# Four stages of a two-layer sequence mixer rearranged: gate columns, forms of h, decay products, adaLN rest

## The chip, the core and the metric

The kernel runs on one core of a Trainium2 chip. The metric is the device time of one execution in microseconds (us). TensorE (PE) multiplies, VectorE (DVE), ScalarE (ACT) and GpSimd (POOL) work element by element, SyncE (SP) issues transfers; GpSimd issues some transfers too, in line with its own instructions. Each engine takes its instructions in a fixed order and waits at the first whose inputs are not there.

## The reference

Two layers of a hybrid mixer over 512 latent and 256 context tokens of width 1024, batch 1, in float32. Each layer: RMSNorm, shift and scale from SiLU(c) (adaLN), one input projection `u = h @ w_in + b_in` whose columns feed two branches and the merge gates, then

```python
rq, rk, rv, rz, mq, mk, mv, mo, mz, mg, gr, gm = split(u)   # 1024 columns each, mg 32
# retention, 8 heads of 128, chunks of 128 tokens, both directions
scores = einsum(qc, kc) * dmat;  inner = scores @ vc
cross  = (qc @ s_prev) * xi                 # xi: the decay of a token in its chunk
# mLSTM, 8 heads of 128, both directions, running-max stabiliser
y_r = headnorm(ret) * silu(rz) @ w_ro;  y_m = headnorm(ml) * silu(mz) @ w_mo
x = x + gate * ((sigmoid(gr) * y_r + sigmoid(gm) * y_m) @ w_out)
```

Latent scans start from the final state of the context. A last RMSNorm gives the output of the latent tokens.

## The kernel before

Every float32 operand of a matmul is split into a high and a low part (`h_hi`, `h_lo`; `w_hi`, `w_lo` in two neighbouring slots of w0 to w3), and a product is three matmuls: high by high, high by low, low by high. A split is a copy by ScalarE (line 180) and a difference by VectorE (line 181), or, for weights under `wsplit`, two ScalarE passes (lines 192, 193) and an accumulating transfer on GpSimd's queue (line 194).

A layer runs through these stages. **gm**: four gate pairs, `gmp{layer}_{j}_256` for the latent and `_0` for the context tokens, each from a pair of weight blocks (gm0, gm2, gm4, gm6) and followed by a tanh on ScalarE into `gmt` (line 621). **Strassen**: the columns of the queries, keys and merge gates as block products `sx`, `sy`, `sz` (line 725). `sy` and `sz` need the forms `t12`, `t34` (sums and differences of four blocks of h), which `make_forms` builds: it loads `fa` and `fb` back from DRAM, forms `fc` and `fd` on VectorE (lines 646 to 649) and splits them. **Retention**: `rvg` (line 281) gives the values of head 0 and 1 and 32 gate columns; `rv0_p` the other values; for each head `rk` (transposes, line 1016), `rs` (scores), the products of queries by decay `xi` into `ws3` (line 1079), `rkv`, `ro`, then `yt_r` (line 1032). **mLSTM**: the same with `mk`, `ms`, `mo`, `yt_m`; the matmuls `mv` (line 274) are its values. Gate columns `gr` (merge gate of the retention branch, in pairs) are spread over these heads: `GRP` says after which retention pair, `GRH` at which mLSTM heads, the rest come after the mLSTM. **br, bm, ou**: branch outputs times gates, and the output projection.

The adaLN parameters (shift, scale, gate: 24 blocks of 128 for each layer) are computed by matmuls at the start for what layer 0 needs first; the rest, `ada_rest`, by VectorE: a block of `in_wadat` is loaded on GpSimd's queue (line 371, four buffers), multiplied by the two rows of SiLU(c) and summed along the row (line 388, result `adj` thrown away, sum kept). For layer 0 blocks 16 to 23 this runs in the retention, in `ws3`, in steps of 256 columns: 8 x 4 steps with two products each, 64 products. For layer 1 it runs after the mLSTM in `gwf`, in steps of 512 columns.

The order is made in two levels. Generators in the list `main` are advanced by `tick()`, those in `side` (the `ada_rest`) by `aside(n)` by n steps, and `drain` runs a list to its end; so calls between the matmul loops decide what is issued where. Over that, a scheduler that works with priorities orders each engine's instructions; code under `tc.high_priority(offset=LOWP)`, with LOWP = -200, is put off.

Of the kernel before, what the change touches and what calls it, by code (L numbers as in the profile page):

```python
# [26 lines left out]
KB = 8  # L27
# [10 lines left out]
LOWP = -200  # L38
# [2 lines left out]
POS = [0, 3, 1, 2, 4, 5]  # L41
KO = [0, 4, 1, 5, 2, 6, 3, 7]
GRP = [(2,), ()]
GRH = [(2, 5), ()]
CTX = slice(0, NCTX)
LAT = slice(NCTX, T)
ROWS = (slice(0, 32), slice(32, 64))
# [18 lines left out]
def build(tc, io):  # L66
# [3 lines left out]
    with ExitStack() as es:  # L70
# [24 lines left out]
        def chunks(t, n=NCH):  # L95
            return t.rearrange("p (n c) -> p n c", n=n)
# [37 lines left out]
        def ensure(key):  # L134
            while key not in finished:
                tick(False)
# [313 lines left out]
        for l in range(NL):  # L450
            def pair(name, a, b, summed=0):
                spec(f"{name}_{l}", wb[l, a], wb[l, b], summed=summed)
            for j in range(0, 8, 2):
                pair(f"gm{j}", B_GM + j, B_GM + j + 1, 2 if j else 0)

            def gr(p):
                pair(f"gr{p}", B_GR + 2 * p, B_GR + 2 * p + 1)
            for p in range(4):
                if p:
                    pair(f"rv{p}", B_RV + 2 * p, B_RV + 2 * p + 1)  # L460
                else:
                    spec(f"rvg_{l}", io["wrvg"][l])
                if l == NL - 1:
                    pair(f"rz{p}", B_RZ + 2 * p, B_RZ + 2 * p + 1)
                    pair(f"rq{p}", B_RQ + 2 * p, B_RQ + 2 * p + 1)
                if p in GRP[l]:
                    gr(GRP[l].index(p))
            if l == NL - 1:
                pair("mq0", B_MQ, B_MQ + 1)
            for h in range(H):  # L470
                pair(f"vo{h}", B_MV + h, B_MO + h)
                if l == NL - 1 and h % 2 == 0:
                    pair(f"mv{h}", B_MV + h, B_MV + h + 1)
                    pair(f"mz{h}", B_MZ + h, B_MZ + h + 1)
                if h in GRH[l]:
                    gr(len(GRP[l]) + GRH[l].index(h))
                if l == NL - 1 and h % 2 and h < H - 1:
                    pair(f"mq{h + 1}", B_MQ + h + 1, B_MQ + h + 2)
            for p in range(len(GRP[l] + GRH[l]), 4):
                gr(p)  # L480
            for nm, summed in (("wro", 2 - 2 * l), ("wmo", 2 - 2 * l), ("wout", 0), ("wout", 0)):
                for p in range(4):
                    spec(f"{nm}{p}_{l}", io[nm][l, 2 * p], io[nm][l, 2 * p + 1], summed=summed)
# [26 lines left out]
        def modulate_ctx(l, x, rst, hp):  # L510
            for i, kb in enumerate(KO):
                modulate(l, x, rst, hp, CTX, kb)
                if i % 3 == 2:
                    yield

        def start_ctx():
            for kb in range(KB):
                square_add(acc, xin[:, kb], kb, CTX)
            rstd_rows(acc, rst, CTX, "ms_inc")
            yield from modulate_ctx(0, xin, rst, hp)  # L520
        main.append(start_ctx())
# [12 lines left out]
        for l in range(NL):  # L534
# [100 lines left out]


            def make_forms(sl):
                n = 256 if sl is LAT else P
                c0 = P if sl is LAT else 0
                for k in range(4):  # L640
                    t0, t1 = stage(f"fa{l}_{k}_{n}"), stage(f"fb{l}_{k}_{n}")
                    for t, kb in ((t0, k), (t1, k + 4)):
                        nc.sync.dma_start(t[:, :2 * n], hd[l][kb][:, sl])
                    (a0, b0_), (a1, b1_) = [(t[:, 0:n], t[:, n:2 * n]) for t in (t0, t1)]
                    f12, f34 = stage(f"fc{l}_{k}_{n}"), stage(f"fd{l}_{k}_{n}")
                    v.tensor_tensor(f12[:, 0:n], b0_, a0, op=OP.subtract)
                    v.tensor_tensor(f12[:, n:2 * n], b1_, f12[:, 0:n], op=OP.subtract)
                    v.tensor_tensor(f34[:, 0:n], b1_, b0_, op=OP.subtract)
                    v.tensor_tensor(f34[:, n:2 * n], a1, f12[:, n:2 * n], op=OP.subtract)
                    for f, tf in ((f12, t12), (f34, t34)):  # L650
                        split(tf[:, 0, :, k, c0:c0 + n], tf[:, 1, :, k, c0:c0 + n], nat2(f[:, :2 * n]))
# [144 lines left out]
            next(first)  # L796
            t12 = big.tile([P, 2, 2, 4, 384], F32R, tag="b3", name=f"t12_{l}")
            t34 = big.tile([P, 2, 2, 4, 384], F32R, tag="b4", name=f"t34_{l}")
            make_forms(LAT)
            next(second)  # L800
            for _ in first:
                pass
            wload(wpos[0])
# [258 lines left out]
            def ret_att(h):  # L1062
# [13 lines left out]
                    v.scalar_tensor_tensor(chunks(sT[0][:, a * P:b * P], w), chunks(ps[:, :w * P], w), SCALE,  # L1076
                                           mk[:, None, :].to_broadcast([P, w, P]), op0=OP.mult, op1=OP.mult)
                for d in range(2):
                    g.tensor_tensor(chunks(qd[d][:, qsl], nq), chunks(qT[:, qsl], nq),  # L1079
                                    xi[d][:, None, :].to_broadcast([P, nq, P]), op=OP.mult)  # L1080
                fetch_qk(h + 2)
                finished.add(("q", l, h))
# [185 lines left out]
            s.activation(zet, zet, AF.Exp)  # L1268
            v.tensor_scalar_mul(zet, zet, SCALE)
            s.activation(rdec, late["lg"][:, l], AF.Exp, scale=float(P))  # L1270
            if need:
                side.append(ada_rest(ws3[:, 3072:4608], 256, [(0, b) for b in range(16, 24)]))
            else:
                rcos, rsin = ws3[:, 3072:3584], ws3[:, 3584:4096]
                nc.sync.dma_start(rcos, io["rope"][0])
                nc.sync.dma_start(rsin, io["rope"][1])
# [4 lines left out]
            for p in range(4):  # L1281
                bt = bias_row(p, f"rv{l}_{p}")
                wv = nextw()
                if p == 0:
                    gtok = gw[:, 3]
                    g.memset(gtok, 0.0)
                    vt = chunks(vts[0][:, :1536])
                    for n in range(NCH):
# [23 lines left out]
                    query(2 * p)  # L1312
                if p:
                    ensure(("w", l, 2 * p - 1))
                main.append(ret_att(2 * p))
                main.append(late_by(3, ret_att(2 * p + 1)))
                if p in GRP[l]:
# [60 lines left out]
                gate_r(w, j, j % 2, G[:, j])  # L1378
            drain(main)
            if l == 0:  # L1380
                side.append(ada_rest(gwf, 512, [(1, b) for k in KO for b in (8 + k, k)]))
            else:
                v.memset(mods[1][:, 16:24, 1], 0.0)
                side.append(ada_rest(gwf, 512, [(1, b) for b in range(16, 24)], (0,)))


            for p in range(4):
                w = nextw()
                for jj in range(2):
                    j = 2 * p + jj  # L1390
                    for ps, sl in proj(w, jj, yr, need, f"br{l}_{j}"):
                        v.scalar_tensor_tensor(G[:, j, sl], G[:, j, sl], 1.0, ps, op0=OP.add, op1=OP.mult)  # L1392
                    if j == 0:
                        ym = (big.tile([P, KB, T], F32R, tag="b0", name=f"ymh{l}"),
                              big.tile([P, KB, T], F32R, tag="b1", name=f"yml{l}"))
                        main.append(reload_split(ymd, ym, f"ym{l}_"))
                    tick(False)
                    tick(False)
                    aside(2)
            drain(main)  # L1400
            y = (big.tile([P, KB, T], F32R, tag="b3", name=f"yh{l}"), big.tile([P, KB, T], F32R, tag="b4", name=f"yl{l}"))
            for p in range(4):
                w = nextw()
                for jj in range(2):
# [9 lines left out]
                    v.tensor_tensor(G[:, j, qsl], G[:, j, qsl], gt[:, qsl], op=OP.add)  # L1414
                    split(y[0][:, j, qsl], y[1][:, j, qsl], G[:, j, qsl])
                    tick(False)
                    aside(3)
            drain(side)


            X = big.tile([P, KB, T], F32, tag="b2", name=f"X{l}")
# [21 lines left out]
            for i, sl in enumerate((LAT, CTX) if need else (slice(256, 512), slice(512, 768))):  # L1443
                n = sl.stop - sl.start
                d = 1 if sl is CTX else 0
                for p in range(4):
                    w = nextw()
                    for jj in range(2):
# [6 lines left out]
                        if need:  # L1455
                            nc.sync.dma_start(x1d[j][:, sl], X[:, j, sl])
                        square_add(acc, X[:, j], j, sl)
                        tick()
                main.append(after(sl, tag, l, need, X, acc, rst, hn if need else None))
            if need:  # L1460
                hp = hn + (True,)
# [77 lines left out]
```

## Time and profile before

| | |
|---|---|
| median of 2 runs | 2166.95 us (2166.61 to 2167.28) |
| profiled execution | 2173.8 us, span 2172.0 us, 34559 instructions |
| TensorE, VectorE, ScalarE, GpSimd busy | 1980.3, 1511.6, 924.4, 553.9 us |
| mean granted TensorE clock | 0.953 of full speed |
| transfers | 335.14 MB, 154 GB/s on the mean |

The profile is one execution. Busy time is a sum over instructions, so it says nothing of where an engine is idle; that is read from windows of the span and from the list of waits. The granted clock is the share of TensorE's full speed in a stretch: at 0.5 (1.2 of 2.4 GHz) a matmul takes twice its time. In a row of the timeline, the bracket is the time in which the engine stood idle before it, and what released it.

### The profile page before, as it was taken

To read this page: it belongs to the slowest core of one execution; us is meant where nothing else is said; L and a number is where in the kernel's file an instruction comes from. 1 tells how busy PE (TensorE), PEld (TensorE's weight loads), DVE (VectorE), ACT (ScalarE), POOL (GpSimd) and SP (SyncE) were. 2 spreads that over 40 slices of the span, in tenths; PEclk is the share of its full clock that TensorE was granted. 3 is DMA by queue.
4 is the path that set the end of the run, shared out by engine and by line. 5 is a ranking of instruction groups with operands and counts; after the bars stand their busy time and mean duration, and the time that the engine had idled before them with its cause. 6 is when DMAs were issued, how large, how long until landed. Compare 5 with 4: busy or idle time off the path is not lost. (4 is left out here: it accounts for less than half of the span.)

```text
span 2172.0 us, 34559 instructions
## 1 busy us (share of the span) xinstructions
PE 1980.3 (91%) x12228; PEld 1829.5 (84%) x12228; DVE 1511.6 (70%) x3512; ACT 924.4 (43%) x1920; POOL 553.9 (25%) x707
## 2 busy tenths in 40 slices
PE   7699999999989669999799986999999999999998
PEld 6589998999878668999688875998798989998788
DVE  6437887876876667876774546997955777776656
ACT  5345555554232224444423364552233444544423
POOL 5231313221223333334131042222122222222100
PEclk9799999999999889999899998999999999999999
DMA  9364655656334424455885676553322334443835
GB/s 330 117 172 132 165 132 152 165 145 183 111 95 146 128 92 160 148 174 148 280 251 129 216 194 191 142 157 107 95 86 86 103 124 142 136 154 112 288 111 173
DMA packets 180940, 335.14 MB, mean 154 GB/s; under 512 B 20704, under 2 KB 63968, under 8 KB 179744
## 3 DMA queue, kind: packets, MB, share of 16 engines
q1 hardware_dynamic: 147552, 239.64, 35.1%
q0 software_dynamic: 33216, 93.30, 16.7%
q8 instruction: 96, 1.57, 0.3%
q14 instruction: 76, 0.62, 0.1%
HBM read 276.28 MB, written 56.58 MB: 153 GB/s over the span
## 5 line engine op out<-in xcount | busy, mean ns | idle before, releaser
L274 PE MATMUL mv<-w_vo,h_hi 128*128 128x256 f32 x1280 | 249.3, 289 | 0.0
L725 PE MATMUL sx<-t,w_st 128*128 128x384 f32 x1152 | 213.9, 336 | 0.0
L274 PEld LDWEIGHTS mv<-w_vo,h_hi 128*128 128x128 f32 x1280 | 203.1, 191 | 1.4
L725 PEld LDWEIGHTS sx<-t,w_st 128*128 128x128 f32 x1152 | 202.5, 189 | 0.1
L274 PE MATMUL mv<-w_vo,h_lo 128*128 128x256 f32 x640 | 185.6, 290 | 0.0
L618 PE MATMUL gmp<-h_hi,w_gm 128*128 128x512 f32 (+1 forms) x384 | 118.4, 392 | 39.1 <-ACT gmt L621 23.8
L274 PEld LDWEIGHTS mv<-w_vo,h_lo 128*128 128x128 f32 x640 | 122.3, 191 | 1.0
L618 PEld LDWEIGHTS gmp<-h_hi,w_gm 128*128 128x128 f32 x384 | 76.6, 214 | 54.4 <-ACT gmt L621 25.0
L274 PE MATMUL rv<-w_rv,h_hi 128*128 128x256 f32 x576 | 112.8, 291 | 1.6 <-DVE ws L1046 1.6
L245 PE MATMUL ou<-yh,w_wout 128*128 128x256 f32 (+1 forms) x512 | 109.1, 310 | 0.0
L258 PE MATMUL br_l<-yrh,w_wro 128*128 128x512 f32 x256 | 92.5, 413 | 11.2 <-DVE G L1392 7.6
L696 POOL DMA_DIRECT2D w_st<-in_wblk x64 | 56.8, 888 | 178.8 <-ACT w_st L695 176.0
L274 PEld LDWEIGHTS rv<-w_rv,h_hi 128*128 128x128 f32 x576 | 92.1, 193 | 2.5 <-DVE ws L1046 2.0
L725 PE MATMUL sz<-t,w_st 128*128 128x384 f32 x384 | 78.1, 351 | 17.6 <-DVE ub L736 16.2
L258 PE MATMUL gr_l<-h_hi,w_gr 128*128 128x512 f32 x256 | 89.8, 408 | 3.8 <-ACT grt L907 2.2
L258 PE MATMUL bm_l<-ymh,w_wmo 128*128 128x512 f32 x256 | 87.9, 394 | 1.9 <-DVE G L1392 1.9
L1079 POOL TENSOR_TENSOR ws<-ws,ws 128x768 f32<-128x768 f32 (+1 forms) x32 | 51.9, 1641 | 146.7 <-PE ro L1129 95.8
L725 PEld LDWEIGHTS sz<-t,w_st 128*128 128x128 f32 x384 | 69.4, 196 | 23.1 <-issue 12.3
L245 PEld LDWEIGHTS ou<-yh,w_wout 128*128 128x128 f32 x512 | 84.0, 191 | 5.1
L274 PE MATMUL rv<-w_rv,h_lo 128*128 128x256 f32 x288 | 83.8, 291 | 0.0
L1186 POOL TENSOR_TENSOR ws<-ws,gw 128x768 f32<-128x768 f32 (+1 forms) x32 | 50.3, 1588 | 119.1 <-PE mo L1237 56.0
L181 DVE TENSOR_TENSOR w_st<-gw,w_st 128x512 fp32r<-128x512 f32 x96 | 68.8, 720 | 16.9 <-ACT w_st L180 16.6
(416 smaller groups left out, 5916.9 us busy)
## 6 DMA issues: line engine op xcount, KB each, us to landing
raw_st<-in_wblk SPq DMA_DIRECT2D x128, 256.0 KB, 3.6
w_st<-in_wblk POOLq DMA_DIRECT2D x64, 256.0 KB, 5.1
raw_vo<-in_wblk SPq DMA_DIRECT2D x64, 256.0 KB, 3.6
raw_wout<-in_wout SPq DMA_DIRECT2D x64, 256.0 KB, 3.6
gw<-grow SPq DMA_DIRECT2D x8, 1536.0 KB, 6.4
gw<-in_wadat POOLq DMA_DIRECT2D x48, 256.0 KB, 4.5
raw_gm<-in_wblk SPq DMA_DIRECT2D x32, 256.0 KB, 5.6
raw_gr<-in_wblk SPq DMA_DIRECT2D x32, 256.0 KB, 3.4
```

What stands on the lines that cost most here:

```text
L181: (eng or v).tensor_tensor(dl, src, dh.bitcast(F32), op=OP.subtract)
L245: pe.matmul(dst, lw[:, j, kb], mv[:, kb, sl], start=first, stop=last)
L258: pe.matmul(lat, lw[:, j, kb], tok(mv[:, kb], LAT), start=first, stop=last)
L274: pe.matmul(dst, sx[:, kb, tk], mv[:, :, kb], start=first, stop=last)
L618: pe.matmul(ps[:, :m], lw[:, jj, kb], hv2(mv[:, kb], sl), start=kb == 0 and lw is w[0] and mv is hp[0], stop=kb == KB - 1 and lw is w[1])
L696: g.dma_start(dl, src(i, o, k), accum_op=OP.add)
L725: pe.matmul(ps[:, :n], w[:, hl, kk * P:(kk + 1) * P], x, start=first and kk == 0 and hl == 0 and x is xh, stop=kk == 3 and hl == 1, skip_g ...
L1079: g.tensor_tensor(chunks(qd[d][:, qsl], nq), chunks(qT[:, qsl], nq), xi[d][:, None, :].to_broadcast([P, nq, P]), op=OP.mult)
L1186: g.tensor_tensor(qd[d][:, qsl], qT[:, qsl], gw[:, 2 + d, qsl], op=OP.mult)
```

## The change

1. `GRH` of layer 0 goes from heads (2, 5) to head (4,); the pair that falls out joins the loop after the mLSTM.
2. The weights of gm2 are split by ScalarE and VectorE like those of gm0, in both layers.
3. The squares of the context tokens for the RMSNorm are issued before the generator `start_ctx` rather than within it.
4. `make_forms` runs under the low priority, and that for the latent tokens is called after the first step of the second gate pair.
5. The retention's decay products (`qd`, 32 instructions) go from GpSimd to VectorE.
6. `ada_rest` of layer 0 goes from the retention to after the mLSTM, ahead of that of layer 1, in steps of 512 columns: 16 steps, 32 products. The numbers of `aside` in br, bm and ou are set anew.
7. The gate columns of the token blocks are gathered in `ktok` instead of `gw`, and `aside(1)` is called in the first retention pair.

```diff
-GRH = [(2, 5), ()]
+GRH = [(4,), ()]
...
-                pair(f"gm{j}", B_GM + j, B_GM + j + 1, 2 if j else 0)
+                pair(f"gm{j}", B_GM + j, B_GM + j + 1, 2 if j > 2 else 0)
...
+        for kb in range(KB):
+            square_add(acc, xin[:, kb], kb, CTX)
+
         def start_ctx():
-            for kb in range(KB):
-                square_add(acc, xin[:, kb], kb, CTX)
...
             def make_forms(sl):
+                with tc.high_priority(offset=LOWP):
+                    forms(sl)
+
+            def forms(sl):
...
+            next(second)
             make_forms(LAT)
-            next(second)
...
-                    g.tensor_tensor(chunks(qd[d][:, qsl], nq), chunks(qT[:, qsl], nq),
+                    v.tensor_tensor(chunks(qd[d][:, qsl], nq), chunks(qT[:, qsl], nq),
...
-            if need:
-                side.append(ada_rest(ws3[:, 3072:4608], 256, [(0, b) for b in range(16, 24)]))
-            else:
+            if not need:
...
-                    gtok = gw[:, 3]
+                    gtok = ktok
                     g.memset(gtok, 0.0)
...
                 if p:
                     ensure(("w", l, 2 * p - 1))
+                else:
+                    aside(1)
...
             if l == 0:
+                side.append(ada_rest(gwf, 512, [(0, b) for b in range(16, 24)]))
                 side.append(ada_rest(gwf, 512, [(1, b) for k in KO for b in (8 + k, k)]))
...
-                    aside(2)
+                    aside(3)
...
-                    aside(3)
-            drain(side)
+                    aside(2)
...
-                        tick()
+                        tick(False)
+                        aside(2)
+                drain(side)
```

The scheduler turns this into other orders. TensorE at the end of layer 0's retention before (`mv` is the fill for the mLSTM, `rk_6` the first step of head 6; the names leave out the layer):

```order
L274 MATMUL mv_2_2_7321<-w_vo_0_6938,h_hi 128x256
L1016 MATMUL rk_6_0_6594<-k_ident,ws_0_4647 128x128 x4
L1016 MATMUL rk_6_4_6600<-k_ident,ws_0_4647 128x128 x2
L1075 MATMUL rs_6_0_6607<-ws_0_4647 128x128 x2
L1075 MATMUL rs_6_2_6611<-ws_0_4647 128x128 x4
L1095 MATMUL rkv_6_0_6623<-ws_0_4648,ws_0_4647 128x256 x2
```

and now, where lines are numbered five further (`rk` is L1021):

```order
L1021 MATMUL rk_6_0_6358<-k_ident,ws_0_4643 128x128 x2
L1037 MATMUL yt_r_5_2_6269<-k_ident,ws_0_4645 128x128
L274 MATMUL mv_1_4_6805<-w_vo_0_6281,h_hi 128x256
...
L274 MATMUL mv_1_0_6879<-w_vo_0_6281,h_hi 128x256
L1080 MATMUL rs_6_0_6371<-ws_0_4643 128x128 x2
L274 MATMUL mv_1_0_6879<-w_vo_0_6281,h_lo 128x256
...
L1080 MATMUL rs_6_2_6375<-ws_0_4643 128x128 x4
```

Before, the last 92 matmuls of `mv0_1_0` and `mv0_2_2` stand ahead of `rk0_6` and none between the steps of heads 6 and 7; now `rk0_6` stands among the last steps of head 5, and the fill between the steps of head 6 and head 7.

ScalarE at the first gate pairs of layer 0 before (`t` are the forms, `gmt_2`, `gmt_3` the activations of the second pair, `w_gm` the weights of the third):

```order
L180 ACTIVATE t_0_746<-fc_2_256_780 128x2x256
L180 ACTIVATE t_0_747<-fd_2_256_781 128x2x256
L621 ACTIVATE gmt_2_256_829<-gmp_2_256_804,hvec_117 128x512
L621 ACTIVATE gmt_3_256_857<-gmp_3_256_832,hvec_117 128x512
L180 ACTIVATE t_0_746<-fc_3_256_794 128x2x256
L621 ACTIVATE gmt_0_0_885<-gmp_0_0_860,hvec_117 128x256
L180 ACTIVATE t_0_747<-fd_3_256_795 128x2x256
L192 ACTIVATE w_gm_0_916<-raw_gm_0_00_918 128x512
```

and now:

```order
L622 ACTIVATE gmt_2_256_769<-gmp_2_256_744,hvec_117 128x512
L431 ACTIVATE h_hi<-xn_3_1_730,mod_116 128x2x128
L431 ACTIVATE h_hi<-xn_7_1_736,mod_116 128x2x128
L622 ACTIVATE gmt_3_256_797<-gmp_3_256_772,hvec_117 128x512
L192 ACTIVATE w_gm_0_912<-raw_gm_0_00_914 128x512
...
L193 ACTIVATE w_gm_0_913<-raw_gm_0_11_929 128x512
L180 ACTIVATE t_0_742<-fc_0_256_804 128x2x256
L180 ACTIVATE t_0_743<-fd_0_256_805 128x2x256
```

The forms stood ahead of the second pair's activations and of the third pair's weights; now they stand behind both. In the same stage TensorE takes `gmp0_5_256` directly behind `gmp0_1_0`; before, `gmp0_2_0` stood between them.

VectorE at the start of layer 0's retention before (`ws2` the values, `gw0` the gathered gate columns, blocks 0 to 3):

```order
L1290 TENSOR_TENSOR ws2_0_4648<-rvg0_2_4756,br_rv0_0_4681 128x256
L1070 TENSOR_SCALAR ws2_0_4648<-ws2_0_4648,zet0_4657 128x2x128
L1290 TENSOR_TENSOR ws2_0_4648<-rvg0_3_4783,br_rv0_0_4681 128x256
L1291 TENSOR_TENSOR gw0_498<-rvg0_0_4702,br_rv0_0_4681 128x4x8
L1291 TENSOR_TENSOR gw0_498<-rvg0_1_4729,br_rv0_0_4681 128x4x8
```

and now (L1293 and L1294 for L1290 and L1291, `ws1` for `ktok`, L1084 the decay products):

```order
L1293 TENSOR_TENSOR ws2_0_4644<-rvg0_3_4779,br_rv0_0_4677 128x256
L1294 TENSOR_TENSOR ws1_0_4643<-rvg0_3_4779,br_rv0_0_4677 128x4x8
L1293 TENSOR_TENSOR ws2_0_4644<-rvg0_4_4806,br_rv0_0_4677 128x256
L1294 TENSOR_TENSOR ws1_0_4643<-rvg0_4_4806,br_rv0_0_4677 128x4x8
L1074 TENSOR_SCALAR ws2_0_4644<-ws2_0_4644,zet0_4653 128x5x128
L1084 TENSOR_TENSOR ws3_0_4645<-ws1_0_4643,ws3_0_4645 128x768 x2
```

Each block's gate columns now follow its values, and the first two decay products stand in VectorE's order before the last block. On GpSimd the memset of the gathered columns stood behind the rope additions of both last query pairs and now stands ahead of both; on TensorE `rk0_0` stood between the first two `rvg` tiles and now stands behind the gate transposes and `rv0_1_2`.

## Rows read from the trace of the kernel before

**Rows 1.** The page's engine totals: busy us, share of the span, instructions.

```profile
PE 1980.3 (91%) x12228; PEld 1829.5 (84%) x12228; DVE 1511.6 (70%) x3512; ACT 924.4 (43%) x1920; POOL 553.9 (25%) x707
```

**Rows 2.** Windows: length, busy PE PEld DVE ACT POOL, PE clock, DMA share, GB/s.

```profile
750.00:800.00 50.00, 23.17 (x132) 20.13 (x133) 38.37 (x158) 13.85 (x43) 16.91 (x22) 0.70 0.24 73
1050.00:1100.00 50.00, 46.03 (x249) 39.49 (x247) 36.71 (x86) 19.89 (x32) 14.60 (x24) 0.93 0.79 250
1100.00:1150.00 50.00, 46.60 (x263) 39.91 (x262) 36.36 (x114) 16.82 (x30) 18.47 (x26) 1.00 0.99 262
1500.00:1550.00 50.00, 47.00 (x292) 41.78 (x291) 48.72 (x96) 12.76 (x27) 7.24 (x5) 0.97 0.28 82
```

**Rows 3.** Waits of PE: for whom, total us, times, longest.

```profile
PE rk L1016 <- DVE adj L388: 25.8, 1, 25.8
PE gmp L618 <- ACT gmt L621: 23.8, 3, 12.8
...
PE rvg L281 <- DVE gw L1291: 10.8, 2, 5.4
```

**Rows 4.** Timeline of PE, end of retention: start, us, instruction, idle before.

```profile
732.62 0.36 PE L274 MATMUL mv<-w_vo,h_lo 128*128 128x256 f32 x1
...
743.62 0.28 PE L274 MATMUL mv<-w_vo,h_hi 128*128 128x256 f32 x1
...
769.75 1.60 PE L1016 MATMUL rk<-k_ident,ws 128*128 128x128 f32 x6 [25.84 <-DVE adj L388]
...
793.75 1.17 PE L1032 MATMUL yt_r<-k_ident,ws 128*128 128x128 f32 x3 [4.81 <-ACT ws L1025]
...
799.55 0.36 PE L274 MATMUL mv<-w_vo,h_hi 128*128 128x256 f32 x1
```

**Rows 5.** Windows of five us behind the stop at 769.75.

```profile
770.00:775.00 5.00, 4.52 (x20) 3.86 (x20) 4.92 (x22) 1.25 (x4) 2.23 (x2) 0.50 0.21 61
775.00:780.00 5.00, 4.39 (x22) 3.60 (x21) 3.16 (x10) 3.58 (x14) 1.36 (x1) 0.82 0.36 114
```

**Rows 6.** Timeline of ACT, gate pairs of layer 0.

```profile
98.62 1.29 ACT L621 ACTIVATE gmt<-gmp,hvec 128x512 f32<-128x512 f32 x2 [0.95 <-DVE t L181]
...
104.63 0.63 ACT L192 ACTIVATE w_gm<-raw_gm 128x512 fp32r<-128x512 f32 x1 [3.32 <-PE gmp L618]
```

**Rows 7.** Timeline of PE, gate pairs of layer 0.

```profile
99.36 0.58 PE L618 MATMUL gmp<-h_hi,w_gm 128*128 128x256 f32 x1 [9.95 <-ACT gmt L621]
...
116.05 1.22 PE L618 MATMUL gmp<-h_hi,w_gm 128*128 128x512 f32 x2 [3.16 <-DMA w_gm<-in_wblk]
```

**Rows 8.** Timelines of DVE and PE, start of layer 1.

```profile
1314.95 0.43 DVE L646 TENSOR_TENSOR fc<-fa 128x256 f32<-128x256 f32 x1 [2.06 <-DMA fa<-hd]
...
1328.39 0.80 PE L618 MATMUL gmp<-h_hi,w_gm 128*128 128x512 f32 x1 [12.80 <-ACT gmt L621]
...
1343.77 2.24 PE L725 MATMUL sz<-t,w_st 128*128 128x384 f32 x12
```

**Rows 9.** Timelines of POOL and PE, start of layer 0's retention.

```profile
549.22 0.73 POOL L1286 MEMSET gw<- 128x768 f32 x1
...
550.67 0.58 PE L281 MATMUL rvg<-w_rvg,h_hi 128*128 128x288 f32 x1 [5.38 <-DVE gw L1291]
```

**Rows 10.** Groups by line: min/median/max ns, first and last start; and one row of DVE's timeline.

```profile
L1079 POOL TENSOR_TENSOR ws<-ws,ws x32: 1267/1800/2631, 556.1 to 1728.3; 128x768 f32<-128x768 f32 x16, 128x512 f32<-128x512 f32 x16
L1069 DVE TENSOR_SCALAR ws<-ws,zet x16: 606/614/3623, 556.5 to 1707.3; 128x640 f32<-128x640 f32 x16
L181 DVE TENSOR_TENSOR yrl<-yr,yrh x16: 685/822/958, 1045.4 to 2030.5; 128x768 fp32r<-128x768 f32 x8, 128x512 fp32r<-128x512 f32 x8
556.52 3.62 DVE L1069 TENSOR_SCALAR ws<-ws,zet 128x640 f32<-128x640 f32 x1
```

**Rows 11.** The adaLN products by line, and GpSimd's loads from 1045 to 1195.

```profile
L388 DVE SCALAR_TENSOR_TENSOR adj<-gw x80: 690/701/747, 1059.3 to 2059.3; 128x512 f32<-128x512 f32 x80
...
L371 POOL DMA_DIRECT2D gw<-in_wadat x28 | 17.3, 620 | 63.5 <-DVE adj L388 55.6 <-DMA gw<-in_wadat 3.6 <-DVE mod L393 3.4
```

## The prediction

> **What bounds the kernel.** I read the engine totals first. TensorE is busy for 91% of the span and VectorE for 70% [rows 1], so a shorter kernel has to come out of TensorE's remaining idle 190 us and out of the stretches at the lower clock; no work of TensorE itself is removed. The windows show where that time lies: not spread out, but in pits. 750 to 800 us holds 23.17 us of matmuls at a granted clock of 0.70, while 1050 to 1150 has TensorE at 46 of 50 with the DMA share at 0.79 and 0.99 [rows 2]. The list of waits then names who ends the pits: one wait of 25.8 us of the retention transposes `rk` for the adaLN products (line 388), 23.8 us of the gate pairs for the activation of line 621, 10.8 us of `rvg` for line 1291 [rows 3]. The change addresses these three.
>
> **The change, part by part.** The sum is made against the profiled execution, 2173.8 us with a span of 2172.0; the median of the runs, 2166.95, is 6.9 us below it. I take the difference worked out below from the median.
>
> *A, the end of layer 0's retention.* All of the `mv` fill is used up at 743.90, then TensorE stands for 25.84 us, then the chain of heads 6 and 7 runs bare with a further stop of 4.81 us, until `mv` fill returns at 799.55 [rows 4]. That is 55.65 us. After the stop the clock stands at 0.50 for five us and at 0.82 for five more [rows 5]: 4.52 x 0.50 + 4.39 x 0.18 = 3.05 us of matmul time lost. The cause is the 64 adaLN products that stand ahead of the heads' instructions on VectorE. In the new order they are gone from there, and `rk0_6` stands at the end of head 5 with `mv0_1_0` and `mv0_2_2` strewn between the steps of heads 6 and 7. Price: at least the stall less what the four retention products of these two heads now cost VectorE, 4 x 0.96 = 3.8 us (0.958 is the longest `yrl` product, which has the same 128x768 shape [rows 10]), so 22 us; at most everything that is not matmul, 55.65 - (23.17 - 3.05) = 35.5. The chain alone took 29.8 us bare (769.75 to 799.55), and the fill, 92 matmuls from 732.62 to 743.90, takes only 11.3, so some idle time inside the chain will stay. I take **-32** (-22 to -36): stall, inner stop, and half of the clock's 3.05.
>
> *B, the start of layer 0.* On ScalarE the activations of line 621 stand behind the forms of h (splits of `fc`, `fd`), so TensorE waits 9.95 us at 99.36 [rows 7] for an activation that starts at 98.62 [rows 6]. Now `gmt0_2` and `gmt0_3` stand ahead of all forms, and the 9.95 go: the slots that the next pair needs come free 9.95 sooner than the 104.63 of before [rows 6], at 94.7. The first matmul out of them was at 116.05, 11.4 us after, with 24 matmuls of `gmp0_2_0` done in between [rows 7]; it can now be at 106.1. But in the new order `gmp0_5` stands directly behind `gmp0_1_0`, so those 24 (2.9 us at 11.3 / 92 each, the same shape [rows 4]) are still to do then, and a stop of some 8 us stands in place of 3.16, with a longer stretch at half clock behind it, for which I take 1.5 us. 9.95 - 2.9 - 1.5: **-6** (-10 to +3).
>
> *C, the start of both retentions.* `rvg` waits 5.38 us in layer 0 [rows 9] and as long in layer 1 (10.8 us, 2 times [rows 3]). It waits for line 1291, and that for the memset of `gw`, which GpSimd reaches only at 549.22 [rows 9] because a rope addition stands ahead of it. The target is now the buffer of `ktok`, the memset stands two rope additions earlier, and on VectorE line 1291 follows line 1290 token block by token block. Both stops go, with about 2 us of clock each (after the stop of A a five us window at 0.50 lost 2.3 [rows 5]): -15. Against it: `rk0_0` may fill `ktok` only after the gate transposes, so head 0 starts later; two transposes wait for the last columns. I give 3 us for that: **-12** (-16 to -8).
>
> *D, the start of layer 1.* The same activation ends a stop of 12.80 us at 1328.39, but the first product of the forms (`sz`) is only at 1343.77, and the forms wait for their loads: the first begins at 1314.95 after 2.06 us of waiting for `fa` [rows 8]. The gate pairs will be done 12 us sooner and then TensorE will stand before `sz`. What remains is the split of gm2: 4 accumulating DMAs and 4 ScalarE passes less against 4 VectorE differences; 0.69 us is the short end of the same `yrl` row, a 128x512 [rows 10]. **-4** (-10 to +2).
>
> *E, gate columns.* One pair leaves the mLSTM heads and comes back at the end; TensorE's work is the same. Cover for it: the other pair still in the loop. **0** (-4 to +5).
>
> *F, the adaLN products after the mLSTM.* 32 products of 128x512 at 0.70 us [rows 11], 22.4 us of VectorE, some 27 with the read-outs of the sums and their additions (an estimate), and 16 loads of 256 KB beside the 28 that are already there [rows 11], on the queue of GpSimd in which the accumulating weight loads also stand. VectorE has 36.7 and 36.4 of 50 in that stretch [rows 2], so it has room for most; the DMA share of 0.99 has none. 16 loads are 4.2 MB, at the 262 GB/s of 1100 to 1150 16 us of transfer, most of which can go to 1150 to 1250. **+4** (0 to +14).
>
> *G, the decay products on VectorE.* 16 x 0.96 + 16 x 0.69 = 26.4 us come to VectorE, and 16 x 1.80 + 16 x 1.27 = 49.1 us leave GpSimd [rows 10]. Part comes back at once: line 1069 took 3.62 us instead of its median of 0.61 when it began at 556.52, just behind the first of GpSimd's products at 556.1 [rows 10]. The trace has this only in single rows, so layer 0 gets nothing; in layer 1, where VectorE is at 48.72 of 50 in 1500 to 1550 [rows 2], 16 x 0.69 = 11 us are added and a quarter of it shows. **+2** (-5 to +10). The Trainium skill, "SBUF — State Buffer", Who interferes with whom, has VectorE and GpSimd take a shared port pair as an exclusive lock, whose loser blocks fully. The row at 556.52 agrees; if all of GpSimd's products had cost VectorE their own length on the path, the term would be 26.4 - 49.1 = -23 and the forecast 2094.
>
> Sum: -32 - 6 - 12 - 4 + 0 + 4 + 2 = **-48**, so 2166.95 - 48 = **2119 us**.
>
> **Rivals.** 2% of the time, about what a measurement can tell from no change, is 43 us: under 2123.6 is faster by more.
> - *The start gives back what it gains, and the adaLN work is dear* (0.17). B and D at 0, F at +14: -32 - 12 + 14 + 2 = -28, **2139**. For it: the slots' 11.4 us and the DMA share of 0.99 [rows 2]. Against it: the loads are spread by a fixed number per block.
> - *The tail is bound by VectorE* (0.11). If heads 6 and 7 go no faster than the bare chain, A is -22 and G +10: -22 - 6 - 12 - 4 + 4 + 10 = -30, **2137**. VectorE had 38.37 of 50 there [rows 2], but with the adaLN products among them. [...]
> - *The forms at low priority become the bound* (0.04). If ScalarE and VectorE get to the forms only when two gate pairs are through, the first `sz` of each layer waits for a whole set. In layer 1 the set took from 1314.95 to 1343.77 [rows 8], 29 us. Both sets bare are +58; with B and D, -10, out of the sum: -38 + 58 = +20, **2187**, slower than before, and by over 2% (2210) only with F and G at their upper ends. It decides once 38 of the 58 us lie bare. Against it: in the new order the forms still stand ahead of the activations of the third gate pair, so at least two pairs' matmuls cover them.
> - *The small losses of the heads go too* (0.18): A -36, B -10, C -16, D -10, F +4, G -5 = -73, **2094**. For it: rows like the one at 556.52.
> - That a move is not made I give nothing: the order shows each.
>
> The forecast keeps 0.50, from 2105 to 2136 (B, D, F and G each by half their bounds). The range reaches the first two rivals and most of the last: **2088 to 2146**; outside lie a third of the last, the forms' case and the end of the first, 0.15 in all. Faster by over 2%: 0.37 of the forecast's 0.50 (most of it lies below 2123.6) and the 0.18, together 0.55. Slower by over 2%: 0.02. Within: 0.43.
>
> **What will show it.** A: no wait of `rk` over 5 us in layer 0, clock above 0.9 in the stretch. B: a stop before `gmp0_5` of about 8 us behind a DMA. C: no wait of `rvg` for line 1291. D: a wait of `sz` or `sx` for the forms of about 8 us in layer 1. F: more idle time before `br_l`. G: line 1069 without its 3.6 us. I am wrong if the 25.8 us come back as waits of heads 6 and 7, or if the br stretch grows by more than 14 us.

## The result, and the profile after

The changed kernel takes 2135.2 us (2134.45 to 2135.96, 2 runs) against 2166.95: a ratio of 0.9854 with an interval of 0.9811 to 0.9896. Timed again in five rounds beside the kernel before it stands at 0.9823 (0.9803 to 0.9843), 2140.38 us against 2176.07. The kernel before has medians of 2171.76 to 2176.07 in four sets of nine runs, so its first two runs lie at its low end, and the gain is about 38 us of 2176. The forecast of 2119 was a gain of 48.

The page's totals of the changed kernel, first its span:

```profile
span 2132.6 us, 34374 instructions
PE 1974.3 (93%) x12228; PEld 1824.4 (86%) x12228; DVE 1512.7 (71%) x3468; ACT 919.6 (43%) x1904; POOL 489.9 (23%) x651
```

Against [rows 1] TensorE's idle time is 158 us in place of 192, and its busy time 6 us less for the same 12228 matmuls, at a mean granted clock of 0.966 in place of 0.953. VectorE's total is unchanged although it took over the decay products; more on that in the experiments. Windows of the changed kernel, columns as in [rows 2]:

```profile
750.00:800.00 50.00, 49.15 (x392) 48.28 (x393) 34.70 (x107) 19.10 (x53) 16.80 (x18) 0.97 0.46 147
1000.00:1050.00 50.00, 39.48 (x188) 32.45 (x188) 31.23 (x60) 23.90 (x39) 8.59 (x13) 0.83 0.91 292
1050.00:1100.00 50.00, 47.51 (x271) 41.03 (x270) 34.84 (x110) 15.88 (x29) 20.19 (x31) 1.00 0.92 263
1450.00:1500.00 50.00, 43.82 (x270) 38.94 (x268) 48.74 (x90) 12.05 (x26) 4.35 (x3) 0.98 0.24 75
```

The pit at 750 is gone (49.15 of 50 at 0.97). The start of br, now at 1004.6, has a pit of its own at 0.83, and there is one at 1450 to 1500 with VectorE at 48.74. What TensorE waited for, by the list of waits:

```profile
PE sz L730 <- DVE ub L741: 17.1, 9, 4.0
PE gmp L619 <- DMA w_gm<-in_wblk: 14.4, 3, 8.8
PE yt_r L1037 <- ACT ws L1030: 13.9, 5, 4.3
PE br_l L258 <- DVE G L1398: 10.1, 3, 5.0
...
PE yt_m L1037 <- ACT ws L1030: 7.7, 1, 7.7
PE sx L730 <- ACT gmt L622: 6.2, 1, 6.2
...
PE gd L988 <- DVE g_x L984: 5.0, 1, 5.0
```

All three waits of [rows 3] that the change addressed are gone: no `rk`, no `rvg` for the gate columns, no `gmp` behind its activation. Three new ones stand in the list: `gmp` for its weights, 8.8 us in one piece; `sx` for the activation, 6.2; `gd` for VectorE, 5.0.

A way to add this up without the waits is to follow the same matmul through two traces. The gain so far, in us, is the start of the first matmul of a name (where the table says so, of the last) in the kernel before, less the same in the changed one:

| place | before | after | gain so far | adaLN move alone | its gain so far |
|---|---|---|---|---|---|
| first `sz`, layer 0 | 139.7 | 129.0 | 10.7 | 135.9 | 3.8 |
| first `sx` | 155.1 | 149.1 | 6.0 | 151.3 | 3.8 |
| first `rvg` | 522.2 | 518.2 | 4.0 | 519.5 | 2.7 |
| first `gr` columns | 619.5 | 611.0 | 8.5 | 615.8 | 3.7 |
| first `mk` (mLSTM) | 797.4 | 753.1 | 44.3 | 755.8 | 41.6 |
| first `br` | 1045.4 | 1004.6 | 40.8 | 1003.8 | 41.6 |
| first `bm` | 1124.4 | 1088.5 | 35.9 | 1082.5 | 41.9 |
| first `ou` | 1193.7 | 1155.1 | 38.6 | 1151.2 | 42.5 |
| last `sx`, layer 1 | 1462.1 | 1421.0 | 41.1 | 1421.2 | 40.9 |
| last `rvg` | 1487.5 | 1438.8 | 48.7 | 1446.2 | 41.3 |
| last `rz` | 1662.3 | 1619.1 | 43.2 | 1621.0 | 41.3 |
| end | 2172.0 | 2132.6 | 39.4 | 2130.5 | 41.5 |

The changed kernel gains 36 us between the first `gr` columns and `mk`, and 7.6 at `rvg` of layer 1; it gives back 8.4 from `mk` to `bm`, and 5.5 in layer 1's retention. Each column is one execution; how far two executions of one program lie apart in such a table is shown further down. The column of the adaLN move alone is the first experiment: one step of 38 us, and no other.

### The profile page after: what moved, and what is told of

Same layout as the page of the kernel before. It is cut to its first block, busy times and chain, and to the rows that moved or that the text cites. A ratio compares the mean times of both kernels' runs of the same rounds, so it can differ in the third digit from the quotient of the medians.

```text
span 2132.6 us, 34374 instructions
## 1 busy us (share of the span) xinstructions
PE 1974.3 (93%) x12228; PEld 1824.4 (86%) x12228; DVE 1512.7 (71%) x3468; ACT 919.6 (43%) x1904; POOL 489.9 (23%) x651
## 5 line engine op out<-in xcount | busy, mean ns | idle before, releaser
L619 PE MATMUL gmp<-h_hi,w_gm 128*128 128x512 f32 (+1 forms) x384 | 112.3, 377 | 22.1 <-DMA w_gm<-in_wblk 14.4
L258 PE MATMUL br_l<-yrh,w_wro 128*128 128x512 f32 x256 | 93.7, 417 | 16.6 <-DVE G L1398 10.1
L730 PE MATMUL sz<-t,w_st 128*128 128x384 f32 x384 | 82.5, 360 | 21.3 <-DVE ub L741 16.8
L388 DVE SCALAR_TENSOR_TENSOR adj<-gw 128x512 f32<-128x512 f32 x112 | 75.5, 708 | 22.1 <-DMA gw<-in_wadat 19.8
L245 PEld LDWEIGHTS ou<-yh,w_wout 128*128 128x128 f32 x512 | 83.9, 191 | 5.7 <-ACT yh L180 0.7
L180 ACT ACTIVATE w_st<-gw 128x512 fp32r<-128x512 f32 x96 | 60.2, 628 | 56.8 <-PE sx L730 40.5
```

Of the source, the lines that this page charges most:

```text
L180: s.activation(dh, src, AF.Copy)
L245: pe.matmul(dst, lw[:, j, kb], mv[:, kb, sl], start=first, stop=last)
L258: pe.matmul(lat, lw[:, j, kb], tok(mv[:, kb], LAT), start=first, stop=last)
L388: v.scalar_tensor_tensor(junk, bufs[n % 4], 1.0, rows[:, d], op0=OP.mult, op1=OP.mult, accum_out=(part if q else m)[:, d:d + 1])
L619: pe.matmul(ps[:, :m], lw[:, jj, kb], hv2(mv[:, kb], sl), start=kb == 0 and lw is w[0] and mv is hp[0], stop=kb == KB - 1 and lw is w[1])
L730: pe.matmul(ps[:, :n], w[:, hl, kk * P:(kk + 1) * P], x, start=first and kk == 0 and hl == 0 and x is xh, stop=kk == 3 and hl == 1, skip_g ...
```

## The experiments

Each ran in five rounds beside the kernel before; ratios are to it. Two kernels whose ratios lie 0.003 apart are about 6 us apart, and the intervals are 0.0013 to 0.0023 to each side, so a difference of 5 us between two kernels is not clear of the noise by its times alone.

**The adaLN move alone.** The kernel before, with this alone:

```diff
-                side.append(ada_rest(ws3[:, 3072:4608], 256, [(0, b) for b in range(16, 24)]))
...
+                side.append(ada_rest(gwf, 512, [(0, b) for b in range(16, 24)]))
...
-                    aside(2)
+                    aside(3)
```

> The kernel before, with part 6 of the change alone (adaLN rest of layer 0 after the mLSTM, with its new steps). Theory: nearly all of the gain is the stop of 25.8 us before head 6 and what hangs on it. The two traces put that stretch at 35.8 us shorter and the br and bm stretch at 2.8 longer, so 33 us less than before by the traces: 2134 to 2142, and no wait of rk over 5 us at head 6. Rival: it takes the other parts too (decay products on VectorE, other gate columns) to close the stop; then the wait comes back at heads 6 and 7 in another form and the time is 2150 or more.

Measured 2132.84, ratio 0.9809 (0.9789 to 0.9829): no less than the whole change, and a little under the expected 2134. From 700 to 800 its trace has one stop at the end of head 7, and none at head 6; the timeline of its TensorE:

```profile
752.21 1.17 PE L1032 MATMUL yt_r<-k_ident,ws 128*128 128x128 f32 x3 [2.52 <-ACT ws L1025]
```

So the stop of [rows 4] needs no other part of the change to close. And br to `ou` took 147.4 us here against 148.3 before (table: 1003.8 to 1151.2, 1045.4 to 1193.7): 32 products and 16 loads more cost nothing there, though the DMA share in 1050 to 1100 is 0.95 (0.99 in 1100 to 1150 before [rows 2], as far from the start of br):

```profile
1000.00:1050.00 50.00, 43.04 (x216) 36.31 (x216) 35.49 (x78) 27.14 (x46) 9.68 (x15) 0.85 0.81 258
1050.00:1100.00 50.00, 46.54 (x263) 39.97 (x262) 31.79 (x97) 11.52 (x22) 21.23 (x31) 1.00 0.95 259
```

**Decay products back on GpSimd**, in the changed kernel:

```diff
-                    v.tensor_tensor(chunks(qd[d][:, qsl], nq), chunks(qT[:, qsl], nq),
+                    g.tensor_tensor(chunks(qd[d][:, qsl], nq), chunks(qT[:, qsl], nq),
```

> The changed kernel (2135) with the decay products back on GpSimd in both layers. Theory: on VectorE they cost about 6 us in layer 1, where the retention grew by 5.8 us between the traces, and nothing in layer 0: 2129 here, and layer 1's retention shorter by 5 to 6 us. Rival, from the port lock: the blocked rows (line 1069 at 3.6 us, its neighbours at 1.8 to 2.3) come back, and with them waits in the heads of layer 0: 2140 or more.

Measured 2140.75, 0.9844 (0.9823 to 0.9864), against 0.9823 (2140.38) for the changed kernel in the next set of rounds: not distinguishable. The time is the rival's, but so is that of the changed kernel there, and neither mechanism shows: layer 1's retention did not get its 5.5 us back (`rvg` to `rz` 181.1 against 180.3; the stop of 5.05 us at `gd` is gone, but one of 4.47 stands at `q_l`), and line 1069 does not return to 3.6 us (here L1074; its longest is 1.61, the same as in the changed kernel). The changed kernel, and below it with the products on GpSimd:

```profile
L1074 DVE TENSOR_SCALAR ws<-ws,zet x16: 602/612/1610, 543.9 to 1664.5; 128x640 f32<-128x640 f32 x16
L1074 DVE TENSOR_SCALAR ws<-ws,zet x16: 604/612/1614, 543.8 to 1674.6; 128x640 f32<-128x640 f32 x16
```

The time that this trace does lose, 8.7 us, it loses from `bm` to `ou` (75.3 us against 66.6), where no decay product is. In the other 13 traces that stretch takes 66.6 to 69.3 us; why it falls differently here is open.

**Gate columns at heads 2 and 5 again**, in the changed kernel:

```diff
-GRH = [(4,), ()]
+GRH = [(2, 5), ()]
```

> The changed kernel with the gate columns at mLSTM heads 2 and 5 again, so one pair less at its end. Theory: the stretch from the mLSTM's first head to br grew by about 3.5 us between the traces because a pair is missing in the middle; with it back, 2131 to 2132. Rival: the end of the mLSTM needs the pair more than the middle; then the time before br grows instead and the result is 2138 or more. Third: the pair only moves work that TensorE does anyway, 2135.

Measured 2125.29, 0.9779 (0.9757 to 0.9802): 10 us faster than the changed kernel, and faster than all three expectations. The theory had 3.5 of it (`br` starts 4.4 us sooner); another 6.8 come from `br` to `bm` (77.1 us against 83.9). This does not hang on one trace: from the first `mk` to the first `bm` the six traces with the pair at head 4 take 335.4 to 339.3 us, the eight with pairs at heads 2 and 5 324.7 to 328.8. ScalarE at that place in the changed kernel, and below it with the pair back:

```profile
1010.21 0.84 ACT L180 ACTIVATE yrh<-yr 128x768 fp32r<-128x768 f32 x1 [1.20 <-DMA yr<-yrd]
1017.60 1.80 ACT L180 ACTIVATE yrh<-yr 128x768 fp32r<-128x768 f32 x2 [6.55 <-DMA yr<-yrd]
```

```profile
999.32 3.05 ACT L180 ACTIVATE yrh<-yr 128x768 fp32r<-128x768 f32 x4
1008.79 1.81 ACT L180 ACTIVATE yrh<-yr 128x768 fp32r<-128x768 f32 x2 [6.41 <-DMA yr<-yrd]
```

With one pair less at the end the first four tiles of `yr` are there when ScalarE comes to them; with two it waits for the second, third and fourth (1.20 to 1.41 us each), the last splits are 8.8 us later (1017.60 against 1008.79, of which 4.4 is the later start), and TensorE stops longer around the start of br:

```profile
999.38 0.86 PE L1037 MATMUL yt_m<-k_ident,ws 128*128 128x128 f32 x2 [7.69 <-ACT ws L1030]
...
1018.50 0.51 PE L258 MATMUL br_l<-yrh,w_wro 128*128 128x512 f32 x1 [2.70 <-ACT yrh L180]
...
1032.50 0.79 PE L258 MATMUL br_l<-yrh,w_wro 128*128 128x512 f32 x1 [4.98 <-DVE G L1398]
```

(With the pair back they are 5.55, none and 3.79, together 6 us less; the rest of the 10.7 was not followed.) Where the late tiles come from is in the order of ScalarE and SyncE; the changed kernel first, then with the pair back:

```profile
991.69 2.17 ACT L193 ACTIVATE w_wro<-raw_wro 128x512 fp32r<-128x512 f32 x4
994.44 2.63 SPq L1359 DMA_DIRECT2D yr<-yrd  x4
```

```profile
980.23 2.17 ACT L193 ACTIVATE w_wro<-raw_wro 128x512 fp32r<-128x512 f32 x4
982.92 3.50 SPq L1359 DMA_DIRECT2D yr<-yrd  x4
```

The loads of `yr` stand on SyncE behind the second half of the weights of br (`raw_wro`), and that waits for ScalarE to split the first half. With two pairs at the end ScalarE comes to this split later, so the first load of `yr` goes out 10.2 us ahead of br in place of 17.3 (10.1 to 10.6 in all six traces with the pair at head 4, 16.8 to 17.7 in the other eight). That the transfers crowd each other does not show: in the 50 us from the start of br the DMA share is 0.83 in the changed kernel and 0.84 with the pair back.

**Gate columns gathered in gw again**, in the changed kernel:

```diff
-                    gtok = ktok
+                    gtok = gw[:, 3]
```

> The changed kernel with the gate columns gathered in gw again. Theory: both stops of rvg come back, 5.4 us each with 2 us of lower clock each: 2135 + 15 = 2150. Rival: what the buffer of ktok buys at rvg it costs at head 0, which has to wait for the gate transposes (the layer 0 stretch to the first gr columns gained only 4.5 us between the traces); then 2138 to 2142.

Measured 2148.53, 0.9874 (0.9854 to 0.9895): about 11 us slower than the changed kernel. Both stops return, in layer 0

```profile
548.59 0.58 PE L281 MATMUL rvg<-w_rvg,h_hi 128*128 128x288 f32 x1 [5.63 <-DVE gw L1294]
```

and 6.2 us in layer 1. By the table's method it loses 8.5 at `rvg` of layer 1. Up to `mk` it loses 8.4 us, but the changed kernel's second trace, just below, is 7.5 us later there too, so the size in layer 0 is open. The theory stands, less some 3 us.

**The changed kernel again**

> The changed kernel itself, timed in the same rounds as the others: 2135. It sets the step from which the others are read, since the median of the kernel before was 2166.95 over 2 runs and 2174.9 over 9. If the gain is the 39 us that the two traces show, the ratio here is 0.982; if it is the 32 us of the first medians, 0.985.

Measured 2140.38, 0.9823 (0.9803 to 0.9843). The 39 us of the traces are right and the 32 of the first medians were the two quick runs of before. Its span, 2141.4, also shows how much one execution differs from another: its first `rvg` is at 525.4, 7.2 us later than in the trace above, with no instruction changed. A single trace tells 5 us in a stage only where the same row says it in several kernels.

**An empty step in layer 1's gate computation**, in the changed kernel:

```diff
                     s.activation(gw[:, 0, a * P:b * P], ps[:, :(b - a) * P], AF.Copy)
                 yield
+                if l:
+                    yield
```

> The changed kernel with one empty step in layer 1's gate computation behind its transposes, so that the product gd stands one step later on TensorE. In the changed kernel TensorE waits 5.05 us at gd for VectorE (g_x), before it did not wait there, and putting the decay products back on GpSimd did not remove the 5 us of layer 1's retention. Theory: the added aside(1) moves the whole gate chain one step ahead of VectorE: 5 us less, 2130, no wait at gd. Rival: layer 1 is bound by VectorE there (48.74 of 50 us busy) and the stop moves to the next step that needs VectorE: 2135.

Measured 2133.86, 0.9798 (0.9777 to 0.9819): 5.5 us faster, with intervals that overlap. The stop that it was to remove, in the changed kernel (it is the same 5.04 to 5.06 in the two kernels above that also have `aside(1)`, the columns in gw and the gate columns at 2 and 5):

```profile
1500.33 1.00 PE L988 MATMUL gd<-g_x,ones_r 64*128 64x384 f32 x1 [5.05 <-DVE g_x L984]
```

With the empty step there is no wait at `gd`; what is left between 1425 and 1560 is 1.44 and 1.07 us. The traces bear out the size: from the last `rvg` to the first `mk` of layer 1 the six with `aside(1)` and no empty step take 269.4 to 272.1 us, the six with both 263.1 to 267.7, and the two without either 263.2 and 263.8. By the code `aside(1)` is needed, since `ktok` is written again by head 0 (not tried without); but it had moved all later steps of the generator one ahead, and `gd` before VectorE's chain of scans.

**Both together: gate columns at 2 and 5, and the empty step**

> The same with the gate columns at mLSTM heads 2 and 5 again, which gave about 10 us. Theory: the two do not touch each other, 2135 - 10 - 5 = 2120. Rival: VectorE binds layer 1, 2125.

Measured 2123.98, 0.9754 (0.9735 to 0.9773), and a second time, below, 0.9752. Together they gain 0.0069 on the changed kernel, 0.0044 and 0.0025 alone. It is the fastest version that was run.

**Forms at normal priority again**, in the changed kernel:

```diff
-                with tc.high_priority(offset=LOWP):
-                    forms(sl)
+                forms(sl)
...
-            next(second)
             make_forms(LAT)
+            next(second)
```

> The changed kernel with part 4 undone: the forms of h at normal priority and ahead of the second gate pair. Theory: the stops of 9.95 us in layer 0 and 12.8 us in layer 1 come back at the gate pairs, but most of it was given back anyway at w_gm (8.8 us) in layer 0 and at the first sx and sz (6.2 and 2.2 us) in layer 1, so 2 us in layer 0 and 4 in layer 1: 2141. Rival: the whole of both stops counts: 2150 or more. Other rival: nothing, 2135.

Measured 2140.36, 0.9826 (0.9808 to 0.9845): no difference in time. The old stops are back in its trace, 10.23 us here and 9.94 in layer 1:

```profile
92.95 0.58 PE L619 MATMUL gmp<-h_hi,w_gm 128*128 128x256 f32 x1 [10.23 <-ACT gmt L622]
```

and the changed kernel pays elsewhere, for the weights of the third pair and, in layer 1, at the first `sx`:

```profile
96.39 1.22 PE L619 MATMUL gmp<-h_hi,w_gm 128*128 128x512 f32 x2 [8.80 <-DMA w_gm<-in_wblk]
...
1293.06 0.69 PE L730 MATMUL sx<-h_hi,w_st 128*128 128x384 f32 x1 [6.17 <-ACT gmt L622]
```

In layer 1 the changed kernel does not pay all of it back: from the first `ou` to the last `sx` the trace with the forms at normal priority takes 270.4 us, and the eight traces with them at low priority take 264 to 267. What makes up for it is seen in this one trace only: its first `sx` of layer 0 is at 147.0, in the eight at 149.1 to 153.4.

**Only the two parts that carried it.** The kernel before with the adaLN move, the columns in `ktok` with `aside(1)`, and the empty step:

```diff
-                    gtok = gw[:, 3]
+                    gtok = ktok
...
+                else:
+                    aside(1)
```

> The kernel before with part 6 (adaLN rest moved, which alone gave a ratio of 0.9809) and part 7 (gate columns in ktok), and the empty step in layer 1's gates; parts 1 to 5 are left undone. Theory: the change's gain is these two alone, parts 2 to 5 are worth nothing together and part 1 costs 10 us: 0.9809 less 11 us for the two stops of rvg is a ratio of 0.976, 2123, the same as the changed kernel with its gate columns and its empty step put right (0.9754). Rival: the forms, the gm2 split or the decay products carry 5 us or more that only showed as nothing because another part ate it; then this one is at 0.979 or more.

Measured 2124.61, 0.9787 (0.9772 to 0.9801): 5 us better than the adaLN move alone, where 11 were due; the intervals of these ratios are too wide to tell 5 from 11. It is behind the 0.9754 of the kernel that also has parts 2 to 5. The three runs below were to tell why.

**The same with the decay products on VectorE**

> The same with the decay products on VectorE (part 5). Theory: the heads' chains get 2 to 3 us shorter in layer 0 where GpSimd's products blocked VectorE's rows, nothing in layer 1: 2 us faster than the one before. Rival by the sum of the products' times, 26 us onto VectorE: slower by 5 us or more.

Measured 2126.2, 0.979 (0.9777 to 0.9804): no difference. The totals are the finding. Without and with the products on VectorE:

```profile
PE 1964.2 (93%) x12228; PEld 1816.4 (86%) x12228; DVE 1503.7 (71%) x3428; ACT 921.9 (44%) x1912; POOL 549.9 (26%) x691
```

```profile
PE 1967.7 (93%) x12228; PEld 1821.2 (86%) x12228; DVE 1506.2 (71%) x3460; ACT 923.9 (43%) x1912; POOL 498.0 (23%) x659
L1081 DVE TENSOR_TENSOR ws<-ws,ws 128x768 f32<-128x768 f32 (+1 forms) x32 | 27.3, 858 | 9.9 <-PE ro L1131 6.2 <-ACT ws L1059 3.6
```

32 instructions more, 27 us in all, and VectorE is busy only 2.5 us longer: some 25 us of its other instructions' time went with GpSimd's 52. In the changed kernel it is the same, 1512.7 and 1513.6 in its two traces against 1510.6 with the products on GpSimd. None of it shows in the time.

**gm2 split by ScalarE and VectorE, added to the two parts**

```diff
-                pair(f"gm{j}", B_GM + j, B_GM + j + 1, 2 if j else 0)
+                pair(f"gm{j}", B_GM + j, B_GM + j + 1, 2 if j > 2 else 0)
```

> The kernel with parts 6, 7 and the empty step, to which part 2 (gm2 split by ScalarE and VectorE) is added. It stood at 0.9787, the kernel with parts 2 to 5 as well at 0.9754; this tells whether part 2 carries the difference. Theory: yes, the split saves 2 to 3 us at the first gate pairs of each layer, where the accumulating loads were waited for: 0.976 to 0.977. Rival: the difference is spread between calls of the same kernel, and this one stands within 0.001 of the kernel beside it.

Measured 2134.79, 0.983 (0.9808 to 0.9851): 9 us slower, against both theories. Its trace loses 9.8 us from the first `sx` to the first `rvg` (372.4 us against 362.6), far behind the split, 4.4 of it in waits of `sz` for `ub` (17.9 us there against 13.5; over the whole run 20.1):

```profile
PE sz L725 <- DVE ub L736: 20.1, 11, 3.8
```

But the 362.6 are the shortest of all 14 traces. The other three without the split take 365.4 to 368.2 in this stretch, the ten with it 367.8 to 372.4, 4.5 us more on the mean. So about half of the 9.8 goes with the split, and the rest is spread; why the split costs anything so far behind it stays open.

**The fastest version a second time**

> The changed kernel with gate columns at heads 2 and 5 and the empty step, a second time and beside the other: 0.9754 if parts 2 to 5 are worth the 7 us, 0.978 or more if that was spread.

Measured 2117.84, 0.9752 (0.9732 to 0.9772). The ratio came out again to 0.0002. If the two parts alone, run once, are as steady, parts 2 to 5 are worth about 7 us together, give or take 5, though the forms taken out of the changed kernel cost nothing and gm2 put in alone cost 9. The traces have 5 of it at layer 1's start: from first `ou` to the last `sx` 264 to 266 us (1149.7 to 1416.0 and 1151.1 to 1415.5), against 270.7 (1147.7 to 1418.4) with the two parts alone. There it goes with the forms and not with the split: all eight traces with the forms at low priority take 264 to 267 us, all six with them at normal priority 268 to 272, and two of these six have the split. Part 3, the squares, never ran by itself, nor did the forms without the split; what each does in layer 0 is open.

## Why the prediction was right, and where not

The time lies in the range, and the direction was right; the size was 48 where 32 were measured at first and 38 with more runs. The main cause, the 25.8 us stop, was right and is shown by the adaLN move alone; that the total came so near is in part luck, as the terms below show. By its own terms:

- **A, -32: right, somewhat small.** The trace gives 35.8 and the move alone 38 (table, `gr` to `mk`), at the upper bound of 36 and beyond: I had allowed for idle time that would stay inside the chain, and it did not stay. TensorE has 94.85 of 100 us in 700 to 800 in the changed kernel.
- **F, +4: wrong, it is nothing.** 147.4 us for 148.3. The DMA share of 0.99 was no sign that 4.2 MB had no room.
- **C, -12: right in sum.** 11 us are lost when it is undone. But a side effect was not seen: `aside(1)` also costs 5.5 us at `gd`, a place that I did not look at, since the order there differs by a few rows only. "`aside(1)` is called" is an instruction to advance a generator, and everything in that generator moves.
- **E, 0 (-4 to +5): the step that failed.** I priced it by TensorE's work, "the same", and called the pair still in the loop its cover. The cover that mattered was not in the middle but in front of br: the loads of `yr` went out 7 us later against its start, and the stop before `yt_m` grew from 5.64 to 7.69. It cost 10 us.
- **B, -6: wrong, nothing that shows.** The mechanism was as described, and the 8 us stop at `gmp0_5` (8.80) is there; but it gives back all, not half. The first `sx` is at 149.1 to 153.4 in the eight traces with parts 2 to 4, and at 151.3 to 155.1 in the four without any of them. The first rival had that.
- **D, -4: right in its stage.** Layer 1's start is some 5 us shorter in every trace with the forms at low priority. The stop before the first `sx` (6.17, of the 8 named) is there, but for the activation of line 622; for the forms `sz` waits 2.2 us. In the time of the whole kernel the 5 us don't show when the forms alone are undone.
- **G, +2: nothing measurable.** 27 us came to VectorE and 25 went from it, and the time is the same. The sign that I had named, line 1069 without its 3.6 us, says nothing of G, since it came with the products on GpSimd too. The port lock as the Trainium skill has it ("SBUF — State Buffer", Who interferes with whom) agrees with these totals; the forecast of 2094 that went with it was not met, so the lock's time was not on the path. The Trainium skill ("Perfetto Trace Analysis", Optimizing Scalar/DVE Operations) says that a saturated VectorE may hand work to ScalarE or even GpSimd, and adds that between GpSimd and VectorE, which share a read port, this might not help; the equal times of the two pairs (0.9787 and 0.979, 0.9844 and 0.9823) agree.

Summed from what was measured: the adaLN move -42 (2132.84 against 2174.93), C -11, E +10, `gd` +5.5, the rest taken as nothing, is -37.5, and the changed kernel has -38 in five rounds. Each of these terms is uncertain by some 6 us, so that they close this well is luck too. Of the 16 us between forecast and first result, some 7 are the reference: I set the difference against a median of two runs, 6.9 us under the profiled execution; that execution was nearer to the medians of nine. The rest, some 10, is E and `gd`, 15.5, and B and D, 10, and C, 1, less the 16 by which A with F (-42 for -28) and G were better: errors of 26 us one way and 16 the other.

Of the rivals, the first (2139, the start gives back what it gains) came nearest in time and was half right in mechanism: layer 0's start did, the adaLN work was not dear. Of the forms' rival nothing came: the longest wait for them is the 2.2 us.

## What to carry to other kernels

Of seven edits one carried the gain. The 11 us of a second were eaten by a third (part 1, 10 us) and by its own side effect (5.5), and that showed only by undoing them one at a time in the finished kernel: a bundle whose total looks fair can hold a loss of 10 us, and taking both out gave the fastest version (0.9752). When work that "TensorE does anyway" is moved, ask which transfers needed the time before it; when a coroutine is advanced one step, look at each engine's order at all of its later steps. Price a stop only together with the next thing that is late: for the forms in layer 0 that was a load of weights, with a stop of 8.80 us in place of 9.95.

## What the runs showed of the hardware that was not expected

Taking 32 element-wise instructions (52 us) off GpSimd shortened the other instructions of VectorE by 25 us, nearly the 27 us that the same 32 took on VectorE itself. Executions of the same program lie up to 13 us apart within one set of nine runs (the kernel before, 2167.84 to 2180.51) and 16 over all sets (2166.61 to 2183.03); within one program a stage can differ by more than 5 us between two traces, as the first `rvg` of the changed kernel does by 7.2.
